# The delta rule's gate as one seven-part product, with sums of weights made in device memory

## The chip, the cores and the metric

The kernel runs on one core of a Trainium2 chip. TensorE (PE in the profile, with its weight loads as PEld) multiplies matrices and writes PSUM; VectorE (DVE) and ScalarE (ACT) do elementwise work; GpSimd (POOL) does a few tiny operations; SyncE (SP) issues nearly all transfers between device memory and the on-chip memory. Each engine runs its own instructions in an order that is fixed when the program is built, and waits on semaphores for the others. The metric is the time of one execution on the device in microseconds (us), as the median of several runs.

## The reference, cut to what matters

Two layers of a hybrid decoder on 512 tokens of width 1024. Each layer normalises its input, multiplies it by one wide matrix `w_in`, feeds the columns to three branches (a state-space branch "ssd", latent attention "mla", a gated delta rule "gdn"), merges the three outputs by sigmoid gates, multiplies by `w_out`, and adds a feed-forward part. All data is float32.

```python
xn = rmsnorm(x, norm1_g)
proj = xn @ w_in
(ssd_z, ssd_xbc, ssd_dt, mla_cq, mla_ckv, mla_kr, gdn_qkv, gdn_z, gdn_b, gdn_a, gate_logits) = jnp.split(proj, split_at, axis=-1)
...
o = gated_delta_chunked(q, k, v, g, beta)
o = rmsnorm(o, norm_g) * jax.nn.silu(z.astype(jnp.float32).reshape(Bsz, S, GDN_V_HEADS, GDN_HEAD_V))
```

The change concerns `gdn_z`, a product of 512 x 1024 by 1024 x 1024 in each layer, whose SiLU gates the delta rule's output.

## The kernel before, in words

**Products.** A float32 matrix is split in two parts, `hi` (rounded to the matmul's type) and `lo` (the rest). A product is then three matmuls, hi by hi, hi by lo and lo by hi, which `mm3` (L219) issues as a group; `triples` records each group, so that a layer's dense work can be counted in groups. Weights are loaded by `weights` (L165) in pieces of 512 KB (tile `wraw`, two buffers) and split by `split_half` (L156): one copy on ACT (`whi`) and one subtraction on DVE (`wlo`), with four buffers of each. `dense_F` (L225) gives channels by tokens, `dense_T` (L253) tokens by channels.

**A layer.** Attention comes first; the latents are normalised in `latent` (L628), whose root is a POOL instruction in `rsq` (L299). Then `gdn_matrix` makes the delta rule's triangular matrices, `gdn_blocks` and `gdn_inverses` (L964, L993) invert them through device memory, and two `ssd_group` calls run around the projections of the attention. `out_proj` (L616) takes four parts of 32 groups, each a gate (L598) and a product (L603). After the four parts of the ssd projection come two units of `gdn_unit` (L1036), each with queries (16 groups), values (32) and its half of the gate z through `silu_T` (L814, 32 groups), then four chunk steps of the delta rule that solve one after another, and the transposes of its output ("out"). The third branch's gates and projection follow, and then the product by `w_out`.

**Seven-part products.** The products by `w_out` (L1240) and `w_down` (L1378) already use seven half-size products in place of eight, with sums of the weights made by DVE.

**Order.** The source order is a priority; a planner orders each engine's instructions by when it expects their inputs. The table `BEHIND` (L188) corrects it: a key names a step (a matmul, a transpose, a transfer), its number a group of the layer's count, and `hold_steps` (L207) puts the step behind that group (for other engines than PE, behind the split of weights that precedes it). The groups are counted from the end of the latents on: attention 96, the two `gdn_matrix` calls to 128, ssd group 0 to 208, two parts of the attention's projection to 272, ssd group 1 to 352, two more parts to 416, the four parts of the ssd projection to 544.

**Tiles.** The tag `tok` has five buffers: the two inverses, and the token-major tiles of the ssd groups and of the units (`v`, `gz`). `ft`, `ft4`, `eE`, `st`, `wk0` to `wk3` and `gk` are the working tiles of both branches.

Of the kernel before, what the change touches and what calls it, by code (L numbers as in the profile page):

```python
# [10 lines left out]
F32 = mybir.dt.float32  # L11
# [48 lines left out]
def hybrid_kernel(ctx, tc, a, out, depth=2, taps=None):  # L60
# [4 lines left out]
    def mk(pl, shape, dt, tag, bufs=None):  # L65
        return pl.tile(shape, dt, tag=tag, name=f"{tag}_{next(uid)}", bufs=bufs)
# [117 lines left out]
    def step(ins, *key):  # L184
# [3 lines left out]
    BEHIND = {  # L188
        ("solve", 0, 1): 634, ("solve", 0, 3): 669, ("attend", 0, 3): 671, ("solve", 1, 1): 714,
        ("solve", 1, 2): 723, ("solve", 1, 3): 739, ("out", 0, 0): 687, ("out", 0, 1): 691, ("out", 1, 0): 759,  # L190
        (0, "pair", 1): 311, (0, "left", 0): 314, (0, "right", 0): 317, (0, "left", 1): 319, (0, "right", 1): 322,
# [5 lines left out]
        (0, "value", 0, 0, 0): 42, (0, "value", 1, 0, 0): 68, (1, "value", 2, 1, 0): 95, (1, "turnx", 0, 1, 0): 199,  # L197
        (1, "turnx", 0, 1, 1): 199, (1, "gramk", 1, 1): 189, (0, "value", 2, 1, 0): 97, (1, "state", 1, 2): 726,
        (0, "d", 210): 217, (0, "state", 1, 2): 731, (0, "turnx", 1, 1, 0): 328, (1, "decay", 8, 3): 375,
        (0, "turnp", 1, 0, 0): 65, (1, "value", 0, 1, 2): 47, (1, "value", 0, 1, 3): 47, (1, "value", 0, 1, 1): 47,  # L200
        (1, "value", 1, 0, 0): 66, (1, "value", 2, 0, 0): 81, (0, "gram", 1, 1): 362, (0, "decay", 12, 2): 367,
        (1, "gram", 1, 1): 362, (1, "decay", 12, 2): 368, (1, "turnb", 0): 194, ("raw", 0, 1): 784,
        ("raw", 1, 1): 800, ("raw", 1, 0): 816, ("sum", 0): 935, (1, "turn", 0, 0): 878, (0, "turn", 0, 0): 877,
        (0, "d", 37): 32,
    }
# [258 lines left out]
    for ly in range(depth):  # L464
# [570 lines left out]

        def gdn_unit(u, kT, ork, cc, cd, Yt, yh, yl):  # L1036
            hd0 = 16 + 4 * u
# [17 lines left out]
            v = mk(br, [P, T, 512], F32, "tok", 5)  # L1055
            gz = mk(br, [P, T, 512], F32, "tok", 5)
            for i in range(2):
                for j, pj in enumerate(dense_F(weights(w_in, O_GV + (4 * u + 2 * i) * P, 256, D), tiles(256), D, xh, xl)):
# [4 lines left out]
                    for t in range(T):  # L1063
                        step(pe.transpose(ps[:, t * P : (t + 1) * P], vf[:, t * P : (t + 1) * P], ident), "turnv", u, h)
                    dve.tensor_tensor(v[:, :, h * P : (h + 1) * P], ps.rearrange("p (t n) -> p t n", t=T),
                                      bc_last(ork[:, i, :], P), ALU.mult)
            silu_T(br, O_GZ + 512 * u, gz)

            hdec = lambda i, t, h: dec[:, i, t, hd0 + h : hd0 + h + 1]
            ss = mk(sp, [P, T, 4], F32, "gos", 2)  # L1070
            st = None
            for t in range(T):
# [68 lines left out]
                for h in range(4):  # L1141
                    gzh = hv(gz[:, t, :])[:, h]
                    dve.scalar_tensor_tensor(gzh, gzh, ms[:, h : h + 1], hv(o)[:, h], ALU.mult, ALU.mult)
            for c in range(4):
                k = 4 * u + c
                ps = y_bank()
                for t in range(T):
                    step(pe.transpose(ps[:, t * P : (t + 1) * P], gz[:, t, c * P : (c + 1) * P], ident), "out", u, c, t)
                split_gain(yh[k], yl[k], ps, col(g_gdn))
                tap(f"ygdn{k}", f32(yh[k]))  # L1150

        cum[:] = cum_rows(br)
# [396 lines left out]
```

## Time and profile before

| | |
|---|---|
| median of three runs | 2312.34 us (2311.65 to 2312.38) |
| the profiled execution, and its span | 2312.48 us, 2310.7 us |
| granted clock of TensorE | 0.999 |
| matmuls and transposes on PE | 11854 |
| DVE, ACT, POOL busy | 71%, 50%, 3% of the span |
| device memory to and from the core | 222.75 MB, 96 GB/s on average |

The span runs from the first instruction to the last of one execution taken by the profiler; the time beside it includes what lies around. A line of a group reads: source line, engine, operation, written tile <- read tiles, shape, count | busy us, mean ns | idle time before, and what ended it.

### The profile page before, as it was taken

What the parts mean: (1) busy time and instruction counts of PE and PEld (TensorE: products, weight loads), DVE (VectorE), ACT (ScalarE), POOL (GpSimd) and SP (SyncE); (2) the same over time, 40 slices, a digit from 0 to 9 for tenths busy, and PEclk for the clock granted to TensorE, in tenths of its full rate; (3) what the DMA queues carried; (4) which work ended last, traced back from release to release, by engine and by line L of the source; (5) the groups of instructions that cost most, each with busy time, mean ns of one, the idle gap of its engine ahead of it and who ended that gap; (6) DMA issues with size and microseconds to landing.
All of it is one profiled execution on the core that took longest, in us unless ns stands there. A gap on an engine that the chain in (4) does not pass through costs nothing.

```text
span 2310.7 us, 31867 instructions
## 1 busy us (share of the span) xinstructions
PE 2294.9 (99%) x11854; PEld 1900.5 (82%) x11854; DVE 1648.4 (71%) x3202; ACT 1149.0 (50%) x2232; POOL 60.7 (3%) x76
## 2 busy tenths in 40 slices
PE   9999999999999999999999999999999999999998
PEld 7888788888888888888888887888888888888887
DVE  6878885635676878767768799665356768777668
ACT  5655534423444465554656555343234445645546
POOL 0000000000000000000000000000000100000000
PEclk9999999999999999999999999999999999999999
DMA  4222442233224343233132233323333251432241
GB/s 143 79 73 73 128 108 65 82 101 91 82 78 127 115 139 108 66 126 119 39 110 74 71 98 107 92 81 91 93 90 87 78 170 58 146 119 82 92 128 46
DMA packets 197403, 222.75 MB, mean 96 GB/s; under 512 B 30976, under 2 KB 152320, under 8 KB 197248
## 3 DMA queue, kind: packets, MB, share of 16 engines
q1 hardware_dynamic: 197104, 220.64, 31.3%
q8 instruction: 93, 1.52, 0.3%
q14 instruction: 62, 0.51, 0.1%
q10 hardware_dynamic: 144, 0.08, 0.0%
HBM read 204.44 MB, written 11.53 MB: 93 GB/s over the span
## 4 chain that ended last, share of the span: by engine, by line
PE 96%; DVE 2%; ACT 1%; DMA 1%; POOL 0%; issue 0%; SPq 0%; POOLq 0%; ACTq 0%; DVEq 0%
PE acc L221 24%; PE acc L223 24%; PE acc L222 24%; PE sm L223 2%; PE sm L222 2%; PE sm L221 2%; PE sm L869 1%; PE sm L775 1%; PE sm L1117 1%; PE sm L1094 1%; PE sm L1108 1%; PE sm L753 1%; PE sm L756 1%; PE yt L791 0%; PE sm L591 0%; PE sm L875 0%
## 5 line engine op out<-in xcount | busy, mean ns | idle before, releaser
L161 ACT CAST whi<-wraw 128x512 fp32r<-128x512 f32 (+1 forms) x560 | 344.5, 619 | 614.8 <-PE acc L222 423.4
L161 DVE TENSOR_TENSOR wlo<-wraw,whi 128x512 fp32r<-128x512 f32 (+1 forms) x560 | 381.5, 685 | 374.4 <-ACT whi L161 363.4
L221 PE MATMUL acc<-yh,whi 128*128 128x512 f32 (+1 forms) x784 | 305.6, 391 | 0.0
L221 PE MATMUL acc<-xh,whi 128*128 128x512 f32 (+1 forms) x784 | 305.4, 391 | 0.0
L223 PE MATMUL acc<-xh,wlo 128*128 128x512 f32 (+1 forms) x784 | 305.0, 389 | 0.0
L223 PE MATMUL acc<-yh,wlo 128*128 128x512 f32 (+1 forms) x784 | 304.5, 389 | 0.0
L222 PE MATMUL acc<-yl,whi 128*128 128x512 f32 (+1 forms) x784 | 304.3, 388 | 0.0
L222 PE MATMUL acc<-xl,whi 128*128 128x512 f32 (+1 forms) x784 | 303.9, 388 | 0.0
L161 ACT CAST whi<-wr 128x512 fp32r<-128x512 f32 x200 | 124.8, 624 | 131.6 <-PE acc L223 43.2
L222 PEld LDWEIGHTS acc<-xl,whi 128*128 128x128 f32 x784 | 147.4, 188 | 29.8 <-issue 1.2
L221 PEld LDWEIGHTS acc<-yh,whi 128*128 128x128 f32 x784 | 146.9, 188 | 30.4 <-ACT yh L296 1.3
L221 PEld LDWEIGHTS acc<-xh,whi 128*128 128x128 f32 x784 | 147.0, 188 | 30.2 <-ACT xh L296 1.3
L223 PEld LDWEIGHTS acc<-yh,wlo 128*128 128x128 f32 x784 | 147.3, 188 | 29.8 <-issue 0.5
L223 PEld LDWEIGHTS acc<-xh,wlo 128*128 128x128 f32 x784 | 147.4, 188 | 29.4 <-issue 0.5
L222 PEld LDWEIGHTS acc<-yl,whi 128*128 128x128 f32 x784 | 147.4, 188 | 29.3 <-issue 1.0
L161 DVE TENSOR_TENSOR wlo<-wr,whi 128x512 fp32r<-128x512 f32 x200 | 137.1, 689 | 35.8 <-ACT whi L161 34.9
L811 DVE SCALAR_TENSOR_TENSOR cva<-acc,pc,cva 128x511 f32<-128x511 f32 (+2 forms) x168 | 119.5, 743 | 19.5 <-ACT cva L809 12.3
L223 PE MATMUL acc<-whi,yl 128*128 128x512 f32 (+2 forms) x312 | 119.7, 384 | 0.0
L222 PE MATMUL acc<-wlo,yh 128*128 128x512 f32 (+2 forms) x312 | 119.6, 383 | 0.0
L221 PE MATMUL acc<-whi,yh 128*128 128x512 f32 (+2 forms) x312 | 119.5, 385 | 0.0
L222 PE MATMUL acc<-wlo,xh 128*128 128x512 f32 (+1 forms) x280 | 107.8, 385 | 0.0
L223 PE MATMUL acc<-whi,xl 128*128 128x512 f32 (+1 forms) x280 | 107.6, 385 | 0.0
(481 smaller groups left out, 4572.0 us busy)
## 6 DMA issues: line engine op xcount, KB each, us to landing
wraw<-in_w_in_dram SPq DMA_DIRECT2D x140, 512.0 KB, 3.7
wraw<-in_w_up_dram SPq DMA_DIRECT2D x64, 512.0 KB, 3.7
wr<-in_w_down_dram SPq DMA_DIRECT2D x32, 1024.0 KB, 5.1
wraw<-in_w_mla_out_dram SPq DMA_DIRECT2D x16, 512.0 KB, 3.5
wraw<-in_w_ssd_out_dram SPq DMA_DIRECT2D x16, 512.0 KB, 3.5
wraw<-in_w_gdn_out_dram SPq DMA_DIRECT2D x16, 512.0 KB, 3.4
wr<-in_w_out_dram SPq DMA_DIRECT2D x8, 1024.0 KB, 6.5
wraw<-in_uq_n_dram SPq DMA_DIRECT2D x8, 512.0 KB, 3.7
```

The costliest lines, as they stand in the source:

```text
L161: pair = act.copy(hi, raw), dve.tensor_tensor(lo, raw, f32(hi), ALU.subtract)
L221: step(pe.matmul(o, ah, bh, start=start, stop=False, skip_group_check=more), "d", len(triples))
L222: pe.matmul(o, ah, bl, start=False, stop=False, skip_group_check=more)
L223: triples.append(pe.matmul(o, al, bh, start=False, stop=stop, skip_group_check=more).ins.name)
L753: step(pe.matmul(o, qh[:, tok], kh[:, :n], start=True, stop=False), "score", hp, j, t)
L756: step(pe.matmul(o, qps[j][:, tok], kps[:, :n], start=False, stop=False), "rope", hp, j, t)
L775: step(pe.transpose(ps[:, n : n + P], pn[t][:, kb * P : (kb + 1) * P], ident), "turnp", hp, j, kb)
L811: dve.scalar_tensor_tensor(acc[:, d:], ps[:, : S - d], taps_[3 - d], acc[:, d:], ALU.mult, ALU.add)
L869: step(pe.matmul(py[:, h * 64 : (h + 1) * 64], e2[h // 4][:, h % 4, :], xd[:, h * 64 : (h + 1) * 64], start=True, stop=True), "scan", g, t)
L1094: m = step(pe.matmul(pw[:, h * P : (h + 1) * P], Y[:, h, :], r[:, h * P : (h + 1) * P], start=True, stop=True), "solve", u, t)
L1108: step(pe.matmul(pS[:, i * 256 : (i + 1) * 256], ktok[i][:, t, :], vd[:, i * 256 : (i + 1) * 256], start=True, stop=True), "state", u, t)
L1117: step(pe.matmul(po[:, h * P : (h + 1) * P], pt_[:, h, :], vn[:, h * P : (h + 1) * P], start=True, stop=True), "attend", u, t)
```

## The change

The gate of both units becomes one product of 512 tokens by 1024 channels, in seven parts of 256 tokens x 512 rows x 512 channels. `z_weights` makes four blocks of combined weights in device memory (`d_w`): SP copies four blocks of `w_in`, and POOL issues seven transfers that add further blocks to them. Nothing holds these steps. `z_operands` makes four combinations of the halves of xn (two token halves by two row halves) on DVE and ACT, in working tiles that are free then. `z_products` runs the seven products in four banks, three blocks of weights straight from `w_in` and four from `d_w`, in loads of 512 KB into `wraw` and, in turn, `bA` and `bB`; it adds the results and applies the SiLU. The gate of unit 0 stays on chip, that of unit 1 goes to device memory (`d_z`) and comes back in its unit.

The order of the layer changes with it: ssd projection part 0, operands, part 1, products, unit 0, part 2, unit 1, part 3, and then the output transposes of both units (`gdn_out`), as their tiles are free only after part 3. The numbers in `BEHIND` behind the products fall by 8, those for unit 0's output rise, and holds for the operands, for the ssd group's output transposes and for some steps of the units are new.

```diff
-        ("solve", 0, 1): 634, ("solve", 0, 3): 669, ("attend", 0, 3): 671, ("solve", 1, 1): 714,
-        ("solve", 1, 2): 723, ("solve", 1, 3): 739, ("out", 0, 0): 687, ("out", 0, 1): 691, ("out", 1, 0): 759,
+        ("solve", 0, 1): 626, ("solve", 0, 3): 661, ("attend", 0, 3): 663, ("solve", 1, 1): 706,
+        ("solve", 1, 2): 715, ("solve", 1, 3): 731, ("out", 0, 0): 700, ("out", 0, 1): 704, ("out", 1, 0): 751,
...
+        (0, "d", 37): 32, ("zop", 0): 430, ("zop", 1): 440, ("zop", 2): 454, ("zop", 3): 466,
+        (0, "gramq", 1, 0): 681, (1, "gramq", 1, 0): 691, (1, "outs", 0, 1, 0): 407, (1, "outs", 0, 1, 1): 407,
...
-        def gdn_unit(u, kT, ork, cc, cd, Yt, yh, yl):
+        def gdn_unit(u, gz, kT, ork, cc, cd, Yt):
...
-            gz = mk(br, [P, T, 512], F32, "tok", 5)
+            if gz is None:
+                gz = mk(br, [P, T, 512], F32, "tok", 5)
+                sync.dma_start(gz, d_z)
...
-            silu_T(br, O_GZ + 512 * u, gz)
...
+        def z_weights(ly):
+            blk_ = lambda i, j: a["w_in"][ly][512 * i : 512 * (i + 1), O_GZ + 512 * j : O_GZ + 512 * (j + 1)]
+            o = [d_w[i].rearrange("k p n -> (k p) n") for i in range(4)]
+            for i, j in ((0, 0), (1, 0), (2, 1), (3, 0)):
+                sync.dma_start(o[i], blk_(0, j))
+            for i, x in ((0, (0, 1)), (2, (1, 1)), (1, (0, 1)), (3, (0, 1)), (1, (1, 1)), (3, (1, 1)), (3, (1, 0))):
+                pool.dma_start(o[i], blk_(*x), accum_op=ALU.add)
+
+        def z_operands():
...
+            def plus(n, x, y, op, k):
+                o, q = w(n), w("gQ" if n == "gk" else "gk")
+                step(dve.tensor_tensor(o, f32(x[0]), f32(y[0]), op), "zop", k, n)
+                dve.tensor_tensor(q, f32(x[1]), f32(y[1]), op)
+                dve.tensor_tensor(o, o, q, ALU.add)
+                return o
+
+            def put(x, s):
+                act.copy(x[0], s)
+                dve.tensor_tensor(x[1], s, f32(x[0]), ALU.subtract)
+
+            for k in range(4):
...
+                s = plus("gQ", a21, a22, ALU.subtract, k)
+                put(s1[k], s)
+                for x in a11:
+                    dve.tensor_tensor(s, s, f32(x), ALU.subtract)
+                put(s2[k], s)
+                q = w("gk")
+                dve.tensor_tensor(q, f32(a12[0]), s, ALU.add)
+                dve.tensor_tensor(q, q, f32(a12[1]), ALU.add)
+                put(s4[k], q)
+                put(s3[k], plus("gk", a11, a21, ALU.subtract, k))
+            return s1, s2, s3, s4
...
+            def product(ps, ops, src, start):
+                nonlocal n
+                for k0 in (0, 2):
+                    raw = raws(n)
+                    n += 1
+                    i = sync.dma_start(raw.rearrange("p (k n) -> p k n", k=2), src(k0)).ins
+                    splits.append((len(triples), {i.engine: i.name}))
+                    for k in (k0, k0 + 1):
+                        hi, lo = split_half(raw[:, (k - k0) * 512 : (k - k0 + 1) * 512])
+                        for t in range(2):
+                            ah, al = (o[:, t * P : (t + 1) * P] for o in ops[k])
+                            mm3(ps[t], ah, al, hi, lo, start and k == 0, k == 3, not start)
...
+            product(x, own(0, 0), block(0, 0), True)
...
+            product(z, own(0, 1), block(1, 0), True)
...
+            product(x, s2, made(1), False)
...
+            product(z, s1, made(0), True)
...
+            product(x, s3, made(2), False)
...
+            product(z, s4, block(1, 1), False)
...
+            product(x, own(1, 1), made(3), False)
+            for t in range(2):
+                silu2(gz[0][:, 2 + t], x[t])
+            sync.dma_start(d_z, gz[1])
+            return gz[0]
...
+        d_w = mk(dr, [4, 4, P, 512], F32, "d_w", 2)
+        d_z = mk(dr, [P, T, 512], F32, "d_z", 2)
...
+        z_weights(ly)
         blocks = gdn_blocks(nts)
...
-        out_proj(a["w_mla_out"][ly], 1, *y_mla, (2, 3))
-        out_proj(a["w_ssd_out"][ly], 0, *ys)
+        out_proj(a["w_mla_out"][ly], 1, *y_mla, (2,))
+        out_proj(a["w_mla_out"][ly], 1, *y_mla, (3,))
+        out_proj(a["w_ssd_out"][ly], 0, *ys, (0,))
+        zs = z_operands()
+        out_proj(a["w_ssd_out"][ly], 0, *ys, (1,))
+        gz = z_products(*zs)
+        gz = [gdn_unit(0, gz, *mats[0])]
+        out_proj(a["w_ssd_out"][ly], 0, *ys, (2,))
+        gz.append(gdn_unit(1, None, *mats[1]))
+        out_proj(a["w_ssd_out"][ly], 0, *ys, (3,))
         yg = hilo_tags(lp, out_tags)
         for u in range(2):
-            gdn_unit(u, *mats[u], *yg)
+            gdn_out(u, gz[u], *yg)
```

More of the change, by code (lines that the diff above doesn't have):

```diff
@@ L1143, in gdn_unit, with gdn_out @@
                     dve.scalar_tensor_tensor(gzh, gzh, ms[:, h : h + 1], hv(o)[:, h], ALU.mult, ALU.mult)
+            return gz
+        def gdn_out(u, gz, yh, yl):
             for c in range(4):
@@ new lines, in z_operands @@
+        def z_operands():
+            tok = mk(br, [P, T, 512], F32R, "tok", 5)
+            places = [[mk(br, [P, 512], F32R, f"wk{k}") for k in range(4)], [tok[:, k] for k in range(4)],
+                      [mk(br, [P, 512], F32R, n, 2) for n in ("eE", "eE", "st", "st")],
+                      [mk(br, [P, 512], F32R, n, b) for n, b in (("ft", 6), ("ft", 6), ("ft4", 2), ("ft4", 2))]]
+            s2, s1, s3, s4 = ([(x[:, HALVES[0]], x[:, HALVES[1]]) for x in p] for p in places)
+            w = lambda n: mk(br, [P, 256], F32, n, 2)
+            def plus(n, x, y, op, k):
[8 more added lines that the diff above has]
+            for k in range(4):
+                a11, a12, a21, a22 = ((xh[4 * j + k][:, HALVES[i]], xl[4 * j + k][:, HALVES[i]]) for i in range(2) for j in range(2))
+                s = plus("gQ", a21, a22, ALU.subtract, k)
[9 more added lines that the diff above has]
+            return s1, s2, s3, s4
@@ new lines, in z_products, with block, made, gate @@
+        def z_products(s1, s2, s3, s4):
+            gz = [mk(br, [P, T, 512], F32, "tok", 5) for _ in range(2)]
+            x, z = ([acc_bank() for _ in range(2)] for _ in range(2))
+            own = lambda i, j: [(xh[4 * j + k][:, HALVES[i]], xl[4 * j + k][:, HALVES[i]]) for k in range(4)]
+            raws = lambda n: mk(wp, [P, 1024], F32, "wraw", 2) if n % 2 == 0 else mk(tl, [P, 1024], F32, "bA" if n % 4 == 1 else "bB")
+            n = 0
+            def product(ps, ops, src, start):
[10 more added lines that the diff above has]
+                            mm3(ps[t], ah, al, hi, lo, start and k == 0, k == 3, not start)
+            def block(i, j):
+                return lambda k0: w_in[(4 * i + k0) * P : (4 * i + k0 + 2) * P, O_GZ + 512 * j : O_GZ + 512 * (j + 1)].rearrange("(k p) n -> p k n", p=P)
+            def made(i):
+                return lambda k0: d_w[i, k0 : k0 + 2].rearrange("k p n -> p k n")
+            def gate(o):
+                t_ = mk(tl, [P, S], F32, "cva", 2)
+                act.activation(t_, o, AF.Tanh, scale=0.5)
+                dve.scalar_tensor_tensor(o, t_, 1.0, o, ALU.add, ALU.mult)
+            product(x, own(0, 0), block(0, 0), True)
+            for t in range(2):
+                act.copy(gz[0][:, t], x[t])
+            product(z, own(0, 1), block(1, 0), True)
+            for t in range(2):
+                dve.tensor_tensor(gz[0][:, t], gz[0][:, t], z[t], ALU.add)
+                gate(gz[0][:, t])
+            product(x, s2, made(1), False)
+            for t in range(2):
+                act.copy(gz[1][:, t], x[t])
+            product(z, s1, made(0), True)
+            for t in range(2):
+                act.copy(gz[1][:, 2 + t], z[t])
+            product(x, s3, made(2), False)
+            for t in range(2):
+                dve.tensor_tensor(gz[1][:, 2 + t], gz[1][:, 2 + t], x[t], ALU.subtract)
+                gate(gz[1][:, 2 + t])
+            product(z, s4, block(1, 1), False)
+            for t in range(2):
+                dve.tensor_tensor(gz[1][:, t], z[t], gz[1][:, t], ALU.subtract)
+                gate(gz[1][:, t])
+            product(x, own(1, 1), made(3), False)
+            for t in range(2):
+                silu2(gz[0][:, 2 + t], x[t])
+            sync.dma_start(d_z, gz[1])
+            return gz[0]
```

15 lines of the change are left out of this document (10 added, 5 removed).

## The prediction, made before the changed kernel was timed

> **What bounds the kernel now.** I read the busy times first, then the chain of waits, then TensorE's waits, then the stages that the change touches. The page's span and busy times, and its chain by engine:
>
> ```profile
> span 2310.7 us, 31867 instructions
> ...
> PE 2294.9 (99%) x11854; PEld 1900.5 (82%) x11854; DVE 1648.4 (71%) x3202; ACT 1149.0 (50%) x2232; POOL 60.7 (3%) x76
> ...
> PE 96%; DVE 2%; ACT 1%; DMA 1%; POOL 0%; issue 0%; SPq 0%; POOLq 0%; ACTq 0%; DVEq 0%
> ```
>
> TensorE is busy nearly all the time and carries 96% of the chain, so a matmul fewer shortens the kernel unless a new wait takes its place. What one is worth isn't its listed duration, because matmuls overlap. The timeline of PE shows two starts ten matmuls apart, that of ACT two gate activations one projection part apart:
>
> ```profile
> 35.62 0.39 PE L223 MATMUL acc<-yh,xl 128*128 128x512 f32 x1
> ...
> 37.89 0.39 PE L221 MATMUL acc<-yh,xh 128*128 128x512 f32 x1
> ```
> ```profile
> 466.98 0.59 ACT L600 ACTIVATE cva<-acc 128x512 f32<-128x512 f32 x1
> ...
> 488.74 0.59 ACT L600 ACTIVATE cva<-acc 128x512 f32<-128x512 f32 x1
> ```
>
> A matmul is listed with 0.39 us but starts come (37.89 - 35.62) / 10 = 0.227 us apart. A part of an output projection (gates and product, 2 x 16 groups of three matmuls) takes 488.74 - 466.98 = 21.76 us, 0.680 us a group, with no gap. TensorE's own waits, the two longest after the start:
>
> ```profile
> PE acc L221 <- ACT cqh L296: 1.2, 2, 0.6
> PE sm L591 <- DVE sg L589: 1.1, 1, 1.1
> ```
>
> There is next to nothing to win from waits; what can be lost is the cover. So I looked at the stages (windows; the columns are the stretch, its length, busy us of PE, PEld, DVE, ACT and POOL, the granted clock, the DMA share and GB/s). The first two are output projections, where the new operands will be made; the others are the existing seven-part product by w_out, the nearest thing to the new one:
>
> ```profile
> 470.00:490.00 20.00, 20.00 (x90) 16.57 (x89) 7.90 (x12) 5.47 (x9) 0.00 (x0) 1.00 0.33 97
> 490.00:510.00 20.00, 20.00 (x90) 16.53 (x89) 7.38 (x11) 5.00 (x9) 0.00 (x0) 1.00 0.36 106
> ...
> 740.00:760.00 20.00, 20.00 (x90) 16.55 (x89) 16.22 (x28) 8.34 (x17) 0.00 (x0) 1.00 0.98 340
> 780.00:800.00 20.00, 20.00 (x90) 16.57 (x89) 16.98 (x31) 9.66 (x18) 0.00 (x0) 1.00 0.03 9
> 800.00:820.00 20.00, 19.68 (x90) 15.99 (x90) 18.62 (x35) 12.26 (x25) 1.38 (x2) 1.00 0.00 1
> ```
>
> DVE is 38% busy in the projections, (7.90 + 7.38) / 40, and TensorE stays whole with DVE at 81 to 85%; with 93% it loses 0.32 us in 20.
>
> **The matmuls removed.** The gate of both units is now 2 x 4 tiles x 8 row blocks = 64 groups of three; seven products of 2 tiles x 4 row blocks are 56. Eight groups a layer, 24 matmuls, 48 in the kernel: 48 x 0.2267 = 10.9 us, all on the chain. The transposes stay as many as they were; those of unit 0's output move behind the last projection part.
>
> **The work added to DVE and ACT.** By group and form:
>
> ```profile
> L1199 DVE TENSOR_TENSOR fd<-mix,mix 128x256 f32<-128x256 f32 x4 | 1.7, 422 | 0.0
> ...
> L161 DVE TENSOR_TENSOR wlo<-wraw,whi 128x512 fp32r<-128x512 f32 x33 | 22.5, 690 | 16.6 <-ACT whi L161 14.3 <-PE yt L1148 1.2 <-PE acc L223 0.9
> L161 ACT CAST whi<-wraw 128x512 fp32r<-128x512 f32 x33 | 20.2, 622 | 29.6 <-PE acc L222 27.6 <-issue 1.5 <-DMA wraw<-in_w_up_dram 0.4
> L292 ACT CAST xh<-mix 128x256 fp32r<-128x256 f32 x8 | 3.0, 405 | 0.6 <-DVE mix L611 0.5
> L611 DVE TENSOR_TENSOR mix<-mix,cva 128x512 f32<-128x512 f32 x4 | 2.7, 686 | 0.0
> ```
>
> Per layer the operands take 14 half-width DVE operations for each of 4 k: 56 x 0.422 = 23.6 us, and 16 ACT copies x 0.405 = 6.5 us. The splits of weights go from 16 to 28: DVE 12 x 0.690 = 8.3, ACT 12 x 0.622 = 7.5. Six sums of banks, 6 x 0.686 = 4.1 on DVE, and six bank copies on ACT, some 3.6 at the gate activation's 0.59. None of it is in a stage that DVE sets: it runs from group 430 of the layer's count (the hold of the first operand) to the end of the products (480 groups stand before them, they are 56), and 106 x 0.680 = 72 us. DVE's work there is 50 groups of projections at 38%, 13.0; operands 23.6; 28 splits 19.3; sums 4.1; eight gate products 8 x 0.686 = 5.5: 65.5 us, 91%. The nearest row is the one with 93%, and I charge its loss: 72 / 20 x 0.32 = 1.15 us a layer, 2.3 us in all. The bounds: nothing, as at 85%; and at most one ACT copy for each of the 16 splits of operands where DVE waits with weight splits queued behind it, 16 x 0.405 x 2 = 13.0 us.
>
> **The order.** Unit 0's solving steps lose the gate as cover and get the third projection part: both are 32 groups, 21.8 us, with DVE work alike (8 splits and 4 more operations each). Unit 1's likewise gets the fourth part. So the cover is moved, and I cost it at 0; uncovered, unit 0's chain would show as gaps between its solve matmuls. The gate of unit 1 goes to device memory and back, 1 MB each, with the 128 groups (87 us) of the third part and both units' keys and values between.
>
> **Transfers.** The 14 loads of 512 KB for the products come in 56 x 0.680 = 38.1 us, one per 2.72 us, 193 GB/s.
>
> ```profile
> wraw<-in_w_in_dram SPq DMA_DIRECT2D x140, 512.0 KB, 3.7
> ...
> wr<-in_w_down_dram SPq DMA_DIRECT2D x32, 1024.0 KB, 5.1
> ```
>
> A load lands in 3.7 us and four buffers give each 4 x 2.72 = 10.9 us to be loaded and split, and the 340 GB/s of the window above (share 0.98, so 347 at most) is well over 193: 0 us.
>
> The sums of weights, per layer 4 copies and 7 accumulating transfers of 1 MB within device memory, have no row of their own. At 347 GB/s 1.05 MB takes 3.0 us; reading and writing device memory at once can't be quicker, so a copy lies between 3.0 and 6.0, an accumulation (two reads, one write) between 3.0 and 9.0. The products need the first of them some 360 groups, 245 us, after the place in the source, so bandwidth costs nothing there. But the source is not where they run: SP's timeline and its waits have next layer's parameters (L343, written after the w_out product) at 13 us.
>
> ```profile
> 13.06 0.34 SPq L343 DMA_DIRECT2D pc<-in_pcols_dram  x1
> 14.40 0.34 SPq L344 DMA_DIRECT2D prow<-in_prows_dram  x1
> ...
> 28.61 1.25 SPq L174 DMA_DIRECT2D wraw<-in_w_ck_dram  x2
> ```
> ```profile
> SPq L343 <- DMA wr<-in_w_in_dram: 1.0, 1, 1.0
> ```
>
> A transfer that waits for nothing goes out as soon as SP is free, so I expect the copies of layer 0, perhaps of both layers, from 13 us on. The next loads, at 28.61, would land by 33.6 and are split from 43.3 on (a row of DVE below), so four copies (13 + 12 to 24 us) still fit before. What can be delayed is behind POOL, which issues the accumulations and stands still while one waits for its copy or its predecessor. Queued on POOL there are the roots of the latents' norms, L301, and who waits for them is DVE's scaling, L638, and TensorE's transposes, L643:
>
> ```profile
> 41.37 1.11 POOL L301 TENSOR_TENSOR lrs<-lrs,nhalf 128x4 f32<-128x4 f32 x1 [14.69 <-DVE lrs L300]
> 58.37 1.01 POOL L301 TENSOR_TENSOR lrs<-lrs,nhalf 128x4 f32<-128x4 f32 x1 [15.89 <-DVE lrs L300]
> ```
> ```profile
> 43.31 0.52 DVE L161 TENSOR_TENSOR wlo<-wraw,whi 128x352 fp32r<-128x352 f32 x1
> 43.75 0.88 DVE L638 TENSOR_SCALAR mix<-mix,lrs 128x512 f32<-128x512 f32 x2
> ```
> ```profile
> 53.99 1.47 PE L643 MATMUL sm<-ct,mix 128*128 128x128 f32 x12
> ...
> 60.42 0.82 PE L643 MATMUL sm<-ct,mix 128*128 128x128 f32 x6
> ```
>
> The first root may be 53.99 - 44.63 = 9.4 us late, the second hardly at all. With one layer's transfers ahead of the second root, at 3.0 each, 4 + 7 end at 13 + 33 = 46 us and POOL is free. I take this lower end, 0 us: the order of an engine is set by when its inputs are expected, TensorE's waits above show that such expectations have been right to about a microsecond, and an accumulation that is expected late goes behind the root. The upper end, 4 x 6 + 7 x 9 = 87, issues the last at 13 + 78 = 91, 33 us after 58.4.
>
> The Trainium skill has a rule against the lower end: "Collectives: The Full Stack", section "The bandwidth ceiling: the fold count and why AG ≠ RS ≠ AR", says that a reducing transfer runs at half a copy's rate, since its two reads share one ring. By it an accumulation takes about 6 us by estimate, POOL issues the last of layer 0 near 61 us, and the sum below would be 2 us higher; no run here shows it yet.
>
> **Sum.** 2310.7 - 10.9 + 2.3 = 2302.1 us of span; the profiled execution took 2312.48, 1.8 more than its span, and the median of the runs is 2312.34. So 2312.34 - 8.6 = 2303.8 us.
>
> **The rivals.** Slower, the roots: if the transfers of both layers stand ahead of the second root on POOL, even at 3.0 us each 8 + 14 end at 13 + 66 = 79, the last is issued at 76, and TensorE stands 18 us; at the upper end for one layer it stands 33. That gives 2322 to 2337, say 2329. It decides against the change from 8.6 us of delay. For it speaks L343's place, 800 us ahead of its source; against it, that the planner has to expect 14 chained transfers within 45 us. Slower too, the loads: if the products' weights came one buffer ahead only, each of 14 would be late by 3.7 - 2.72 = 1.0 us, 28 us in all, 2331; the four buffers and 340 GB/s speak against it.
>
> No change, the operands: if half or all of the 13.0 us bound is paid, the sum is 2312.3 - 10.9 + 6.5 to 13.0, 2308 to 2314.5, say 2310. For it speaks DVE at 91%, against it the 85% rows with TensorE whole; it decides where DVE has splits behind an operand's wait.
>
> Faster than forecast: with no loss on DVE (2301.5) and the two waits of TensorE shown first closed by the moved holds (2.3 us), 2299.2.
>
> That the change leaves the matmul count alone can't be: the loops fix it.
>
> **How the numbers follow.** The forecast has 0.64, the faster case 0.03, the operands 0.17, the roots 0.13, the loads 0.03. About 0.2%, 4.6 us, is what the measurement can tell from none: up to 2307.7 is faster, from 2317.0 slower. Of the operands' case 0.03 is on the fast side and 0.14 within; so faster 0.70, same 0.14, slower 0.16. The range goes from 2298.5 (just under the faster case) to 2320: it leaves out the two slower cases, 0.16. The forecast's own range is 2301.5 (no loss) to 2307.
>
> **What would show it.** PE's count 11854 - 48 = 11806; the copies on SP near 13 us; POOL's two roots at 41.4 and 58.4, or later by what TensorE then waits; 56 half-width operations a layer near 0.42 us with PE at 20.00 in the windows of the products; the loads of the products 2.7 us apart. The forecast is wrong if TensorE has a wait over 2 us in the first 100 us, or PE windows under 19.5 between the operands and the last product.

## The result and the profile after

The changed kernel takes 2419.86 us (median of 4 runs, 2418.49 to 2421.30), the kernel before it, on the same chip, 2312.36 (4 runs, 2311.65 to 2314.45). The ratio is 1.0463, with a 95% interval of 1.0445 to 1.0482: slower by 107.5 us, where the forecast was 8.5 faster. The span of the profiled execution went from 2310.7 to 2419.5 us.

The functions stand seven lines further down: the root L301 is now L308, DVE's scaling L638 is L645, the matmuls L221 to L223 are L228 to L230. In some experiments below everything stands one line lower still. From the page of the changed kernel, the span, busy times, TensorE's busy tenths in 40 slices of 60 us, and the new transfers (count, KB each, median us from issue to landing):

```profile
span 2419.5 us, 32052 instructions
...
PE 2287.9 (95%) x11806; PEld 1894.1 (78%) x11806; DVE 1706.9 (71%) x3350; ACT 1179.4 (49%) x2300; POOL 74.4 (3%) x90
...
PE   7039999999999999999999999999999999999998
...
d_w<-in_w_in_dram POOLq DMA_DIRECT2D x14, 1024.0 KB, 8.7
d_w<-in_w_in_dram SPq DMA_DIRECT2D x8, 1024.0 KB, 20.5
```

TensorE has 48 matmuls fewer and 7 us less to do, and stands throughout the second slice. Its longest waits:

```profile
PE acc L229 <- DVE wlo L161: 98.1, 1, 98.1
PE acc L228 <- ACT whi L161: 15.9, 1, 15.9
```

These two waits, 114 us, are more than the 108.8 us by which the span grew. The timeline of POOL shows what it did meanwhile (columns: start, length, engine, line, operation; in brackets the idle time before and what ended it):

```profile
22.30 1.22 POOL L1169 DMA_DIRECT2D d_w<-in_w_in_dram  x1 [7.52 <-DMA d_w<-in_w_in_dram]
...
75.69 1.02 POOL L1169 DMA_DIRECT2D d_w<-in_w_in_dram  x1 [7.72 <-issue]
84.72 1.04 POOL L1169 DMA_DIRECT2D d_w<-in_w_in_dram  x1 [8.01 <-issue]
...
156.52 1.03 POOL L1169 DMA_DIRECT2D d_w<-in_w_in_dram  x1 [7.93 <-DMA d_w<-in_w_in_dram]
157.17 1.47 POOL L308 TENSOR_TENSOR lrs<-lrs,nhalf 128x4 f32<-128x4 f32 x1
```

All fourteen accumulations, those of layer 1 too, stand ahead of layer 0's first latent root. From 66.94 to 156.52 us POOL issues one every 9.0 us on average and does nothing between, and the root comes at 157.17 us instead of 41.37. DVE's timeline shows who waits:

```profile
158.67 0.88 DVE L645 TENSOR_SCALAR mix<-mix,lrs 128x512 f32<-128x512 f32 x2 [101.30 <-POOL lrs L308]
159.47 0.52 DVE L161 TENSOR_TENSOR wlo<-wraw,whi 128x352 fp32r<-128x352 f32 x1
```

The scaling by the root holds up DVE for 101.30 us, and behind it on DVE stands the split of a weight block that TensorE needs next. So TensorE stops in a projection that has nothing to do with the root. In the windows (columns as in the prediction), the clock that is granted falls with it and is not back at once:

```profile
40.00:60.00 20.00, 5.31 (x34) 5.01 (x32) 11.58 (x22) 1.52 (x2) 2.98 (x6) 0.70 0.98 257
...
80.00:100.00 20.00, 0.00 (x0) 0.00 (x0) 0.00 (x0) 0.00 (x0) 2.06 (x2) 0.50 0.77 128
...
160.00:180.00 20.00, 17.48 (x86) 15.98 (x87) 10.78 (x29) 10.01 (x25) 1.01 (x1) 0.82 0.50 125
```

The other wait, 15.9 us, comes from the early transfers. SP's timeline has the copies from 13 us on, and among and behind them the loads of the tile `qh` (constants, then positions) and the next weight loads, at 40.92 us instead of 28.61. Then DVE's and ACT's timelines:

```profile
13.38 4.79 SPq L1167 DMA_DIRECT2D d_w<-in_w_in_dram  x4
...
21.93 8.79 SPq L127 DMA_DIRECT2D qh<-in_cmats_dram  x1
...
40.92 10.72 SPq L174 DMA_DIRECT2D wraw<-in_w_ck_dram  x2
```
```profile
44.44 0.30 DVE L128 CAST am_b<-qh 128x256 bf16<-128x256 f32 x1 [16.01 <-DMA qh<-in_cmats_dram]
```
```profile
56.22 0.72 ACT L147 ACTIVATE sinT<-qh,inv_c 128x512 f32<-128x512 f32 x1 [15.41 <-DVE qh L146]
60.72 0.48 ACT L161 CAST whi<-wraw 128x352 fp32r<-128x352 f32 x1 [3.78 <-DMA wraw<-in_w_ck_dram]
```

DVE stands 16.01 us for the constants and ACT 15.41 us behind DVE; then ACT stands another 3.78 us for the weight load. Either alone would have held up the split that TensorE needs, ACT until 56.9 and the load until 60.7 us.

The product itself gained what it should. POOL's roots on either side of it went from 432.19 to 551.66 us and from 816.42 to 930.48 in layer 0, so the stage became 119.47 - 114.06 = 5.4 us shorter; in layer 1 the delay falls from 114.15 (1579.59 to 1693.74) to 108.8 at the end, 5.35. The windows from the operands to the products keep TensorE whole:

```profile
575.00:595.00 20.00, 20.00 (x96) 16.19 (x95) 17.91 (x43) 11.23 (x22) 0.00 (x0) 1.00 0.31 88
...
sum 80.00, PE 80.00 PEld 65.86 DVE 60.90 ACT 43.20 POOL 0.00; mean PE 20.00 PEld 16.47 DVE 15.23 ACT 10.80 POOL 0.00
```

### The profile page after: what moved, and what is told of

Same layout as the page of the kernel before. It is cut to its first block, busy times and chain, and to the rows that moved or that the text cites. A ratio compares the mean times of both kernels' runs of the same rounds, so it can differ in the third digit from the quotient of the medians.

```text
span 2419.5 us, 32052 instructions
## 1 busy us (share of the span) xinstructions
PE 2287.9 (95%) x11806; PEld 1894.1 (78%) x11806; DVE 1706.9 (71%) x3350; ACT 1179.4 (49%) x2300; POOL 74.4 (3%) x90
## 3 DMA queue, kind: packets, MB, share of 16 engines
q0 software_dynamic: 7392, 14.68, 3.7%
## 4 chain that ended last, share of the span: by engine, by line
PE 90%; issue 4%; DMA 3%; DVE 2%; ACT 1%; POOL 1%; SPq 0%; POOLq 0%; ACTq 0%; DVEq 0%
PE acc L228 23%; PE acc L230 23%; PE acc L229 23%; PE sm L228 2%; PE sm L230 2%; PE sm L229 2%; DMA d_w<-in_w_in_dram 2%; PE sm L876 1%; PE sm L782 1%; PE sm L1124 1%; PE sm L1101 1%; PE sm L1115 1%; PE sm L763 0%; PE sm L760 0%; POOL d_w L1169 0%
## 5 line engine op out<-in xcount | busy, mean ns | idle before, releaser
L228 PE MATMUL acc<-xh,whi 128*128 128x512 f32 (+1 forms) x784 | 306.1, 392 | 0.0
L228 PE MATMUL acc<-yh,whi 128*128 128x512 f32 (+1 forms) x784 | 306.1, 392 | 0.0
L230 PE MATMUL acc<-xh,wlo 128*128 128x512 f32 (+1 forms) x784 | 304.9, 389 | 0.0
L230 PE MATMUL acc<-yh,wlo 128*128 128x512 f32 (+1 forms) x784 | 304.4, 389 | 0.0
L229 PE MATMUL acc<-wlo,xh 128*128 128x512 f32 (+1 forms) x240 | 92.9, 387 | 98.1 <-DVE wlo L161 98.1
L228 PEld LDWEIGHTS acc<-yh,whi 128*128 128x128 f32 x784 | 146.9, 188 | 30.2 <-ACT yh L303 1.3
L230 PEld LDWEIGHTS acc<-yh,wlo 128*128 128x128 f32 x784 | 147.4, 188 | 29.6 <-issue 0.5
L228 PEld LDWEIGHTS acc<-xh,whi 128*128 128x128 f32 x784 | 147.0, 188 | 29.9 <-ACT xh L303 1.3
L230 PEld LDWEIGHTS acc<-xh,wlo 128*128 128x128 f32 x784 | 147.4, 188 | 29.3 <-issue 0.5
L818 DVE SCALAR_TENSOR_TENSOR cva<-acc,pc,cva 128x511 f32<-128x511 f32 (+2 forms) x168 | 119.6, 743 | 19.6 <-ACT cva L816 12.3
L229 PEld LDWEIGHTS acc<-wlo,xh 128*128 128x128 f32 x240 | 45.8, 191 | 106.3 <-DVE wlo L161 98.5
L228 PE MATMUL acc<-whi,xh 128*128 128x512 f32 (+1 forms) x240 | 92.8, 388 | 15.9 <-ACT whi L161 15.9
L229 PE MATMUL acc<-wlo,yh 128*128 128x512 f32 (+2 forms) x272 | 103.7, 381 | 0.0
L230 PE MATMUL acc<-whi,yl 128*128 128x512 f32 (+2 forms) x272 | 103.6, 382 | 0.0
```

What stands on the lines that cost most here:

```text
L228: step(pe.matmul(o, ah, bh, start=start, stop=False, skip_group_check=more), "d", len(triples))
L229: pe.matmul(o, ah, bl, start=False, stop=False, skip_group_check=more)
L230: triples.append(pe.matmul(o, al, bh, start=False, stop=stop, skip_group_check=more).ins.name)
L818: dve.scalar_tensor_tensor(acc[:, d:], ps[:, : S - d], taps_[3 - d], acc[:, d:], ALU.mult, ALU.add)
```

## The experiments

Theory 1 is the reading above: the loss is POOL's order, the root behind the accumulations. Theory 2, the rival, is congestion: the eleven transfers of a layer take bandwidth from transfers that TensorE waits for, wherever POOL's roots stand. Comparisons are with the kernel before on the same chip; where no interval is given, there is one run.

### The seven-part product without its sums

```diff
             def made(i):
-                return lambda k0: d_w[i, k0 : k0 + 2].rearrange("k p n -> p k n")
+                return block(0, 0)
...
-        z_weights(ly)
```

The sums of weights are left out: the products load a block of the weights in their place, so only the transfers within device memory are gone.

> The changed kernel without any copy or accumulating transfer: the four products that use sums of weights read one plain block of the weights in their place (so the sums are left out). The price of the seven-part product alone. Both theories: 2301.5 if DVE's 91% costs nothing, 2303.8 with the 2.3 us that the prediction charged, 2308 or more if operands stall the splits. The difference to the run before is what the sums cost when they are out of the way.

Measured: 2303.44 us, ratio 0.9958 (0.9943 to 0.9972), against the forecast of 2303.8. So the product itself is worth 8.8 us, and the sums cost the rest, 2419.9 - 2303.4 = 116.4 us. Its profiled execution has a span of 2301.7 us. From its timeline of POOL:

```profile
39.33 1.11 POOL L308 TENSOR_TENSOR lrs<-lrs,nhalf 128x4 f32<-128x4 f32 x1 [14.70 <-DVE lrs L307]
...
182.64 0.53 POOL L568 MEMSET wk<- 128x512 f32 x1 [125.29 <-PE sm L782]
```

The root of the changed kernel is 157.17 - 39.33 = 117.8 us late against this one, and the spans differ by 2419.5 - 2301.7 = 117.8. That the two agree to the decimal is chance: at the end of the attention the lag is 303.80 - 182.64 = 121.2 us, and the kernel without sums loses some 3 us of it in the block inverses of layer 1, where it is not a clean yardstick (see below).

### The root moved from POOL to DVE

```diff
-            rsq(rs, ss, 1.0 / width, EPS)
+            dve.tensor_scalar(rs, ss, 1.0 / width, EPS, ALU.mult, ALU.add)
+            dve.reciprocal(rs, rs)
```

The square root is left out (a reciprocal stands in its place); all transfers stay as they are.

> The changed kernel, all transfers where they are, but the latents' root is taken off POOL: a DVE reciprocal stands in its place (so the norm of the latents is left out in part: it divides by the mean square and not by its root). Theory 1, POOL's order: the 14 accumulating transfers stand ahead of the first root on POOL, and TensorE waits for the root. Then the long wait of 98 us goes, and what is left of the delay is that of the copies on SP's queue ahead of the loads of w_ck (a wait of 16 us in the changed kernel): 2312.4 - 10.8 + 16 to 20 = 2318 to 2322. Theory 2, congestion: the transfers themselves hold up the loads of the attention while they run, until 165 us. Then most of the delay stays: over 2360.

Measured: 2341.82 us. Of the 116.4 us, 78 are gone, though the fourteen accumulations still ran early, 10.2 us apart on average (67.70 to 169.24 us). Theory 1 has two thirds of the loss, and is not all. The 38 us that stay arise before the end of layer 0's attention: POOL's memset there comes 222.36 - 182.64 = 39.7 us later than without sums. Some 15 of them are the wait behind the early copies, for which theory 1 allowed 16 to 20; the other 25 arise in the attention, where the accumulations now run beside TensorE's work. From TensorE's waits:

```profile
PE acc L228 <- ACT whi L161: 14.9, 1, 14.9
```

### The accumulations ordered behind the roots

```diff
+            roots.append(rsq(rs, ss, 1.0 / width, EPS).ins.name)
...
-                pool.dma_start(o[i], blk_(*x), accum_op=ALU.add)
+                d = pool.dma_start(o[i], blk_(*x), accum_op=ALU.add)
+                tc.add_manual_dep(d.ins, roots[-1], ..., reason="in_order")
```

> The changed kernel, with each layer's accumulating transfers ordered behind that layer's second latent root on POOL; the eight copies stay early on SP. Theory 1: the roots are on time, the copies' part stays: 2318 to 2322, with one wait of TensorE of about 16 us for the third load of w_ck, and seven transfers about 9 us apart from 75 us on. Theory 2: seven transfers congest the attention of each layer, so a delay of 30 us or more stays in layer 0 and as much appears in layer 1.

Measured: 2338.67 us. The root is back near its place (49.90 us; the copies still delay it by some 10) and 35 us of span stay. By POOL's memset at the end of each layer's attention (205.48 and 1330.52 us, for 182.64 and 1292.48 without sums), 12.3 us are lost in layer 0's attention besides those 10.6, and 15.1 in layer 1's, about half of what theory 2 expected of a layer. TensorE's waits are now short ones in the attention stretch, in both layers; ACT's cast that it waits for is itself kept 15.9 us, in seven pieces, by swaps of the tile "mix":

```profile
PE sm L764 <- ACT qps L735: 12.0, 5, 5.0
PE acc L229 <- ACT whi L162: 9.4, 3, 5.2
```

Where they come from is seen in the issues of transfers between 60 and 130 us, with the median time to landing in the last column. First without sums, then with the accumulations there:

```profile
wraw<-in_mla_w_ukv_dram SPq DMA_DIRECT2D x3, 512.0 KB, 3.6
...
mix<-mix SPq DMA_DIRECT2D x4, 64.0 KB, 2.0
```
```profile
d_w<-in_w_in_dram POOLq DMA_DIRECT2D x7, 1024.0 KB, 9.7
...
wraw<-in_mla_w_ukv_dram SPq DMA_DIRECT2D x2, 512.0 KB, 8.8
...
mix<-mix SPq DMA_DIRECT2D x4, 64.0 KB, 7.1
```

A swap of 64 KB takes 7.1 us for 2.0, a load of 512 KB 8.8 for 3.6. This agrees with the Trainium skill, "DMA: Bandwidth & Descriptors", section "Issuing engines are not separate DMA queues", which says that transfers started by different engines run on the same 16 DMA engines and interleave. Theory 2 is right that this costs, and had its size too large.

### The same, with the copies of each layer apart

```diff
-                sync.dma_start(o[i], blk_(0, j))
+                step(sync.dma_start(o[i], blk_(0, j)), "zw", i)
...
+        ("zw", 0): 2, ("zw", 1): 14, ("zw", 2): 28, ("zw", 3): 42,
```

> As the run before, and the four copies of each layer held behind groups 2, 14, 28 and 42 of that layer, so that one at a time goes out during the attention. Theory 1: both waits go and the matmuls saved are left: 2312.4 - 10.9 = 2301.5, up to 2305 if a load of the attention comes late behind a copy. Theory 2: 2325 or more.

Measured: 2339.28 us, ratio 1.0114 (1.0098 to 1.0131). The first root is back at 39.01 us, so the early copies are no longer in its way, but copies and accumulations now meet in the attention stretch, where a swap of 64 KB takes 10.1 us. By the same memsets, 13.9 us are lost in layer 0's attention and 19.9 in layer 1's. What is won on the one side is lost on the other; as long as the accumulations run in that stretch, the change loses.

### Layer 1's copies held back to layer 1

```diff
+        (1, "zw"): 126,
```

on the copies as above, with the accumulations as in the changed kernel.

> Layer 0 as in the changed kernel, but the copies of layer 1 are held back to that layer, so its seven accumulations stand on POOL behind layer 1's own latent roots and only the seven of layer 0 stand ahead of layer 0's first latent root. POOL's order: the root comes after seven accumulations instead of fourteen, about 95 us instead of 157, so some 62 us of the 116.4 come back and layer 1 pays for its swaps as in the kernel with the accumulations behind the roots (some 13 us): 2419.9 - 62 + 13 = 2371 us (2355 to 2380). Rival (the root is late for another reason than the count ahead of it, such as the copies or the clock): the root stays past 130 us and the time over 2395 us, or it is back before 60 us and the time under 2345 us.

Measured: 2393.78 us, above the first theory's 2380 and just short of the rival's 2395; the root decides between them. For layer 0 the expectation holds: seven accumulations ahead of the root, which comes at 84.75 us (expected 95; the rival had past 130 or before 60). What was not expected is layer 1. There the copies came so late that POOL stood with the seven accumulations in front of the memset at the end of the attention. From POOL's timeline, then DVE's and TensorE's waits:

```profile
1353.33 1.10 POOL L1169 DMA_DIRECT2D d_w<-in_w_in_dram  x1 [105.99 <-DMA d_w<-in_w_in_dram]
...
1414.16 0.94 POOL L568 MEMSET wk<- 128x512 f32 x1
```
```profile
DVE wk L570 <- POOL wk L568: 35.6, 1, 35.6
```
```profile
PE acc L229 <- DVE wlo L161: 34.0, 1, 34.0
PE acc L228 <- DVE cva L818: 31.9, 1, 31.9
```

TensorE's 34.0 us are layer 0's root, its 31.9 us layer 1's memset. It is theory 1 a second time, with another small instruction of POOL: a memset behind seven accumulations, DVE in order behind the memset, TensorE behind DVE.

### What one accumulation costs

Two kernels with POOL's order as in the changed kernel. One accumulates 256 of the 512 rows of each block, so half of each sum is left out; the other issues the fourteen as plain copies, so the sums are left out.

```diff
-                pool.dma_start(o[i], blk_(*x), accum_op=ALU.add)
+                pool.dma_start(o[i][:256], blk_(*x)[:256], accum_op=ALU.add)
```

> The changed kernel with each accumulation over 256 of the 512 rows (0.5 MB for 1 MB), so the lower half of the sums is left out; number and order on POOL as in the changed kernel. If the 8.9 us of one are a price by the megabyte, one takes about 4.5 to 5 us, the first latent root comes at 157 - 14 x 4.2 = about 95 to 100 us and the time is about 2355 to 2365 us. If they are a fixed price of one accumulation on POOL, nothing moves: 2415 to 2425 us.

```diff
-                pool.dma_start(o[i], blk_(*x), accum_op=ALU.add)
+                pool.dma_start(o[i], blk_(*x))
```

> The changed kernel with the fourteen accumulations as plain copies of the same blocks on the same queue of POOL, so the sums are left out. If the addition is what makes one slow (twice the engine time of a copy), one takes 3 to 5 us, the first latent root comes at about 75 to 100 us and the time is 2335 to 2365 us. If the issue on POOL's own queue is what takes the time (its 512 rows of 2 KB by software), they stay 8 to 9 us apart and the time stays at 2410 to 2425 us.

Measured: 2352.50 and 2355.26 us, near what a price by the work moved gives, and the first root at 89.45 and 94.81 us. So neither the count of accumulations nor the issue by itself sets the 9.0 us (8.9 in the expectations). The times alone would not show it, as TensorE's longest wait is another here: 33.9 us in the first kernel and 34.8 in the second, behind the loads of weights and of `qh` as above, and only 13.6 and 17.0 behind the root.

```profile
PE acc L228 <- ACT whi L161: 33.9, 1, 33.9
```

With POOL issuing faster, its transfers and SP's copies now meet: the DMA engines are full from 20 to 60 us (share 1.05 in the first kernel), and the loads land 23.2 us after their issue. So that the times came out as forecast is in part luck, and the price is better read from the engines' time. The transfers of POOL's queue, from the two pages (packets, MB, share of the 16 engines' span), and then the changed kernel between 60 and 156 us, where next to nothing else runs (busy tenths of the DMA engines in 40 slices of 2.4 us, and the queue):

```profile
q0 software_dynamic: 3808, 7.34, 1.9%
```
```profile
q0 software_dynamic: 3808, 14.68, 2.0%
```
```profile
DMA  9923991599099729924990798189529924990798
...
q0 software_dynamic: 5783, 11.48, 72.9%
```

The half accumulations take 0.019 x 2350.7 / 7.34 = 6.1 us of the engines for a MB, the plain copies 0.020 x 2353.5 / 14.68 = 3.2; the changed kernel's 0.729 x 96 / 11.48 = 6.1. An addition costs 1.9 times a copy. That agrees with the rule that the prediction weighed and did not take, that a reducing transfer runs at half a copy's rate, as the page states it for the reduce step of a collective (the Trainium skill, "Collectives: The Full Stack", section "The bandwidth ceiling: the fold count and why AG ≠ RS ≠ AR"). A whole one of 1.05 MB takes 6.4 us by this, and the rest of the 9.0 us is the low slice or two that the row shows after each burst: a landing takes 8.6 us (median in this window), so it looks as if the next were issued when its predecessor has landed. The half accumulations and the plain copies, with 3808 / 14 = 272 packets each for 528, went out in pairs at times. Whether the number of packets decides on that was not tried.

### The accumulations behind the attention and the inverses' memsets

Both prices are known now, so this run asks for a place that pays neither: the copies of a layer at 268 to 313 us, the accumulations behind the last memset of the block inverses, at 327 us, with POOL's next root at 431 us and the first sum needed at some 500.

```diff
+        ("zw", 0): 246, ("zw", 1): 260, ("zw", 2): 274, ("zw", 3): 288,
...
-                pool.memset(xs[u][:32, :, 32:], 0.0)
+                last_set.append(pool.memset(xs[u][:32, :, 32:], 0.0).ins.name)
...
+                for n in last_set[-2:]:
+                    tc.add_manual_dep(d.ins, n, ..., reason="in_order")
...
-        z_weights(ly)
         blocks = gdn_blocks(nts)
+        z_weights(ly)
```

> The sums are complete, as in the changed kernel; only their place is another: the four copies of a layer are issued on SP among the weight loads of about 285 to 315 us, and the seven accumulations of a layer stand on POOL behind the last memset of the block inverses (326.6 us in the kernel without sums), so none stands ahead of a latent root and none runs beside the small swaps of the attention stretch. Theory of two prices (POOL's order, and the swaps of 64 KB in the attention stretch that slow down beside an accumulation): both prices are gone, the latent root is back at 39 us, the next root on POOL (430.5 us) comes after seven accumulations of 8.9 to 9.8 us from 333 us, that is after some 400 us, and the time is that of the kernel without sums plus little: 2303 to 2307 us, faster than before. Rival (the transfers cost wherever they stand, since TensorE also waits for the weight loads beside them, 512 KB from 3.8 to 7.4 us in the attention stretch): some 15 to 35 us stay, 2318 to 2338 us.

Measured: 2311.07 us, ratio 0.9987 (0.9978 to 0.9996). This lies between the theory's 2307 and the rival's 2318. Some 109 us are back, but 6.2 us of span against the kernel without sums stay. Layer 0 is clean (at its end the two differ by 0.45 us); all but 0.3 us of it arises in layer 1 between 1446 and 1582 us. There the inverses' swaps are waited for at once. One of TensorE's waits, then the issues between 1460 and 1500 us, without sums and here:

```profile
PE sm L1016 <- DMA bA<-d_x: 2.5, 2, 1.6
```
```profile
wraw<-in_w_in_dram SPq DMA_DIRECT2D x4, 512.0 KB, 4.3
tok<-d_y SPq DMA_DIRECT2D x8, 64.0 KB, 2.7
```
```profile
wraw<-in_w_in_dram SPq DMA_DIRECT2D x4, 512.0 KB, 7.2
tok<-d_y SPq DMA_DIRECT2D x8, 64.0 KB, 8.2
```

With a second wait of 1.5 us, behind a cast that starts about when its weight load lands (1504 us), the waits are 4.0 of the 6.2 us. In the two windows of 20 us that have these waits, TensorE was granted a clock of 0.91 and 0.83, which may be the rest. The yardstick has such a loss too, without a wait. In the kernel without sums POOL's roots on either side of this stretch are 1575.84 - 1445.75 = 130.1 us apart, in the changed kernel, whose accumulations are long done by then, 1693.74 - 1566.69 = 127.1. The window of the former, with TensorE busy and a clock of 0.83:

```profile
1480.00:1500.00 20.00, 19.93 (x222) 16.10 (x220) 10.86 (x16) 8.32 (x15) 0.00 (x0) 0.83 0.24 80
```

So single executions differ here by some 3 us for a reason that no run separates.

### Later still in layer 1

Two runs set the copy for the first accumulation of layer 1 later, at two places.

```diff
+        (1, "zw", 0): 312,
```

> As the kernel with the accumulations behind the last memset, but in layer 1 the copy that the first accumulation adds to is issued on SP only behind the small swaps of the block inverses and two weight loads (about 1479 us), so the seven accumulations of layer 1 run from about 1485 to 1550 us instead of 1462 to 1530. Theory (the 6.2 us that the kernel before it still lost, all of them in layer 1 between 1460 and 1582 us, are the swaps of 64 KB that took 8.2 us for 2.7 beside an accumulation): the loss of 1460 to 1480 us is gone, 4 to 6 us come back, 2302 to 2306 us, faster than before. Rival (the loss comes from the weight loads, 7.2 us for 4.3 beside the accumulations at 1492 to 1510 us): it stays, 2308 to 2311 us.

The other has 330 for 312.

> As the run before it, with that copy another two loads of weights later (about 1500 us), so the accumulations of layer 1 run from about 1505 to 1570 us, beside neither the swaps nor the three weight loads that follow each other at 1493 to 1504 us. By both theories 2302 to 2305 us; where it stands more than 1.5 us below the run before it, the weight loads have a share of the loss. The next root on POOL (1576 us in the kernel without sums) comes last behind seven accumulations: if they take 10 us and more each it is late by some us, and the time 2305 to 2310 us.

Measured: 2307.63 us, ratio 0.9976 (0.9967 to 0.9985), and 2309.85 us, 0.9989 (0.9980 to 0.9998). The edit did not do what the expectations say: the planner put accumulations whose copies stood ready in front of the late one, and in both runs POOL issued from 1462 us on, beside the swaps. So the times do not test the two places. But the second run's trace speaks for the rival. With two accumulations issued beside the swaps, which land in 7.7 us, 1460 to 1480 us is whole, and TensorE's one long wait is behind a weight load at 1500 us:

```profile
1460.00:1480.00 20.00, 19.99 (x253) 16.22 (x252) 9.77 (x14) 5.63 (x10) 3.16 (x4) 1.00 1.05 184
```
```profile
PE sm L1041 <- ACT eE L1038: 3.9, 1, 3.9
```

The next two keep the written order as well.

```diff
+                last_set.append(d.ins.name)
```

> In the two runs before this one only the first named accumulation of layer 1 was late; the other copies stood ready and theirs still ran from 1462 us beside the swaps. Here the seven accumulations of a layer also keep their written order on POOL, so that in layer 1 all seven come behind the copy that SP issues behind the swaps (1479 us): from about 1485 to 1550 us. Theory (in layer 1 the swaps beside the accumulations cost): the stretch of 1460 to 1480 us is as in the kernel without sums, and of the 6.2 us that were lost at first 3 to 6 come back: 2303 to 2307 us. Rival (the weight loads at 1492 to 1506 us, which TensorE has used up by then, cost as well): the time stays at 2306 to 2310 us, and TensorE stands in 1500 to 1520 us.

> As the run before it, but the copy that the seven accumulations of layer 1 follow is issued behind the weight loads of 1492 to 1500 us, so they run from about 1503 to 1570 us. Theory and rival agree here: no swap and no run of weight loads is beside them, TensorE is busy throughout 1460 to 1520 us, and the time is that of the kernel without sums plus at most 2 us: 2302 to 2306 us. If the weight loads are what costs, this one is 2 to 5 us below the run before it; if the accumulations cost in any place, it stays at 2306 to 2311 us.

Measured: 2309.13 us, ratio 0.9986 (0.9976 to 0.9995), and 2305.22 us, 0.9970 (0.9958 to 0.9981). The windows of 1460 to 1480 and of 1500 to 1520 us of the former, then the second window of the latter:

```profile
1460.00:1480.00 20.00, 19.85 (x253) 16.09 (x252) 9.54 (x14) 5.72 (x10) 1.03 (x2) 1.00 0.77 193
...
1500.00:1520.00 20.00, 16.57 (x96) 14.01 (x95) 5.61 (x9) 8.03 (x13) 2.63 (x3) 0.74 0.90 207
```
```profile
1500.00:1520.00 20.00, 20.00 (x134) 16.16 (x133) 9.90 (x15) 10.29 (x18) 2.12 (x2) 1.00 0.86 198
```

Behind the swaps, 1460 to 1480 us is nearly whole, but TensorE now stands 3.4 us in the stretch where it needs weight loads that follow each other. TensorE's wait and ACT's timeline of the former show the link:

```profile
PE sm L1041 <- ACT eE L1038: 3.4, 1, 3.4
```

```profile
1501.89 0.62 ACT L162 CAST whi<-wraw 128x512 fp32r<-128x512 f32 x1 [6.75 <-DMA wraw<-in_w_in_dram]
...
1503.13 0.58 ACT L1038 COPY eE<-sm 64x512 f32<-64x512 f32 x1
```

ACT waits 6.75 us for a load, and the copies behind it on ACT are what TensorE's solve waits for. Behind those loads too, both stretches are whole (19.95 us of TensorE in the first); a wait of 1.5 us is left between 1520 and 1540 us, and the span is 2301.9 us.

In these executions, then, the rival was right: the weight loads cost, in each of the four kernels where the accumulations ran beside them (1.5 to 3.9 us of waiting; in two of the four the load is read from its landing just before the cast), and the swaps less surely (2.5, 0.9 and no wait in the three where they ran beside those). What the place is worth in time is shown less well. The former kernel's times run from 2303.3 to 2313.7 us, three of its twelve below 2304; the profiled execution of the latter, 2303.71 us, is the fastest of five; and the intervals overlap. So does that of the first run of the pair before, so the last kernel can't be told from it. Against the kernel before the change it stands clear: it computes all sums, has the lowest median of those that do, 2305.22 us, and is 0.3% faster.

## Why the prediction was wrong

**The matmuls.** 48 fewer were costed at 10.9 us. They were 48, and the two stages became 5.4 and 5.35 us shorter: right.

**DVE and ACT.** 2.3 us were charged for DVE at 91%. Over the four windows of that stage DVE is busy 60.90 of 80 us, 76%, and even where it has 90% TensorE is whole: the term measured 0. That the sum of -8.6 us of span comes so near the -9.0 of the kernel without sums is luck: between POOL's roots and the end, its two stages are 5.5 and 5.25 us shorter, and it loses 2.6 against the kernel before in layer 1's inverses (130.1 us for 127.5), a loss that the prediction doesn't have.

**The moved cover and the loads**, costed at 0, show no wait of TensorE: right.

**The transfers.** This is the step that failed: "I take this lower end, 0 us", with its reason that "an accumulation that is expected late goes behind the root". The planner put all fourteen ahead of the first root. TensorE's waits, from which the trust in its expectations was drawn, show how well it knows engines; they say nothing of transfers within device memory, of which the kernel before has none. In place of 0 the term measured 116.4 us.

**The price of one** lay at the upper end of the bounds given: 9.0 us from one issue to the next, for 3.0 to 9.0. The half rate of the Trainium skill ("Collectives: The Full Stack", the section named above) gave an estimate of about 6, which is the transfer alone (6.4 measured).

**The rival "roots"** had the place and the mechanism, and a price of 18 to 33 us. It priced both layers at the lower end and one layer at the upper, but never both layers at the upper end. By its own bounds that is 13 + 8 x 6 + 14 x 9 = 187 us to the end and the last issue at 178, some 120 us after 58.4; measured was the last issue at 156.5. It named the second root; it was the first that was held up. And the victim was not the transposes of the latents, which left the first root 9.4 us, but a weight split that stands behind the scaling on DVE.

**The early copies.** "Four copies still fit before" looked at the weight loads alone. Eight went out, and the loads were issued 12.3 us late, with the wait of 15.9 us. With only four early, in the run that held layer 1's back, the loads were issued in time (26.58 us), and yet TensorE waited 8.5 us there: now behind the constants in `qh`, for which DVE waited 12.4. Accumulations ran beside these copies, so what four alone cost is open.

**What no case held** is the second cost: swaps of 64 KB and weight loads that take two to four times as long beside an accumulation. Without the waits behind the early copies, it is some 25 to 34 us in the three kernels whose accumulations ran beside the attention (39.7 - 14.9, 12.3 + 15.1 and 13.9 + 19.9) and up to 6 of span where they ran beside layer 1's inverses, and doesn't show in the changed kernel, where TensorE stood while they ran.

## What to carry to other kernels

Where a transfer is issued by an engine that also does small work on the path, look at what stands behind it in that engine's order, and price the case that all such transfers of the program stand ahead of it, at the upper bound of each. A transfer with 240 us of slack is not free for that: its place has to be given, both on the engine that issues it and among the transfers that others wait for. When an ordering hint is used, look in the timeline at whether it held: two runs here moved one transfer and the planner let the others pass.

## What the runs showed of the hardware

- An accumulating transfer of 1 MB within device memory takes 6.4 us of the 16 DMA engines, 1.9 times a copy, and POOL issued the next only 9.0 us after it, near the 8.6 us of its landing. The idle time is put down to "issue", not to a transfer.
- Beside one accumulation at a time, swaps of 64 KB went from 2.0 to 7.1 us and loads of 512 KB from 3.6 to 8.8, while the share of the DMA engines in windows of 20 us was only 0.59 to 0.88; in layer 1's inverses, where it was 1.04 and 0.88, swaps went from 2.7 to 8.2.
- TensorE's granted clock was 0.50 in the stall and 0.82 in the window after it; a matmul of 128x352 was listed with 0.66 us at the restart, for 0.32 before it. A window of the kernel without sums had a clock of 0.83 with TensorE busy 19.93 of 20 us and no wait listed; no run shows why.
